# Writing an mLSTM stage with its gate projections ahead of its convolved queries and keys

## Chip, core and metric

The kernel runs on one core of a Trainium2 chip. The metric is device time in microseconds of one execution. Inputs and outputs lie in HBM and are float32; products run on TensorE (PE), elementwise work on VectorE (DVE), ScalarE (ACT) and GpSimd (POOL), and nearly all DMAs are issued from SyncE's queue (SP).

## What is computed

One step of a two-layer decoder trunk, for 1024 new tokens of one prompt and for one new token of each of 8 running sequences (the "samples"). Each layer projects its input `x` (1024 channels) once and feeds three groups of heads: mLSTM (M), retention (R) and HGRN2 (H). Their gated outputs go through one output projection and a LayerNorm.

```
qk        = silu(causal_conv(m_qk))                       # width 4, on the q and k of the mLSTM group
(C, n, m) , h_m = chunked mLSTM(q, k, v, gates)           # matrix memory per head, carried on
y_m       = head_layer_norm(h_m) * sigmoid(m_o) * silu(m_z)
y_r       = head_layer_norm(retention(rope(q), rope(k), v)) * silu(r_g)
y_h       = head_rms_norm(hgrn2(...)) * silu(h_g)
x         = layer_norm(ALPHA * x + W_out [y_m | y_r | y_h])
```

`sigmoid(m_o) * silu(m_z)` are the two gate paths of the mLSTM group. They need only `x`, like every other input projection; what they give is multiplied with the normed heads at the very end.

## The kernel before

The tokens lie along the free dimension, the channels on partitions, and they are worked in two halves: b = 0 holds 512 prompt tokens and the 8 samples (520 columns), b = 1 the other 512. The program writes out, in this order, the stages H, R and M of a half and later its output projection; the stages of the next half lie between. A stage is named here by (layer, half): M of (0, 0), of (0, 1), of (1, 0) and of (1, 1), which is last.

A projection (`project`, L140) makes 128 output channels. Its weights come in two tiles of 256 KB (`load_w`, L126): a DMA, an ACT cast (L133) and a POOL subtraction (L134) split them into a high and a low part; three buffers hold them. Then PE issues 24 products for each run of columns: two runs of 260 columns for b = 0, one of 512 for b = 1. A PSUM tile `pp` (three buffers) takes the sum and a small function `use` evicts it.

The R stage ends with a loop over four chunks of 128 tokens (L474 to L504): transposes (L479, L484), scores (L489), a mask on DVE (L492), outputs (L496, L497), the state (L500, L502), a norm on DVE (L169 to L183, with a power on POOL at L162), and transposes and a product into the gated tile (L206, L212). For b = 0 eight sample steps follow (`sample_R`, L754): each loads a state and two broadcast rows by DMA into `smp` tiles (four buffers), multiplies on POOL (L762), updates on DVE (L763), stores, multiplies on POOL again (L707) and reduces on DVE (L708).

The M stage (`in_M`, L515) has 15 projections. Six give q and k: ACT copies them out (L539), DVE applies the convolution in four passes (L551, three times L553), ACT takes a tanh (L555), DVE finishes the silu (L557), and a DMA moves 32 rows to another tile (L562). `load_x` (L567) then loads the input of the next stage: DMA, ACT cast, DVE subtraction (L157). Three projections give the values (L570). Six are the gate paths, `gate_paths` (L572): an ACT tanh and one DVE operation for each run of columns (L219 and L579). The tiles `tmp` for conv, load and gates come from one ring of four buffers. Four chunks of 128 tokens follow (L591 to L646), beginning with the transposes of values (L604) and keys (L610), and for b = 0 eight sample steps of their own (`sample_M`, L810; L823 and L708 on DVE).

The instruction order on each engine is not that of the text: a scheduler of the tile framework places instructions by readiness and by their place in the program, before the run. At run time each engine takes its instructions strictly in that order. For M of (1, 1) the gate paths are written after the chunks (`final`), in both kernels.

## Time and profile before

| | |
|---|---|
| median of 3 runs | 1415.11 us (1412.8 to 1416.36) |
| the profiled execution | 1413.7 us, span of the core 1411.9 us |
| granted clock of TensorE, mean | 0.968 |
| busy share: PE, DVE, POOL, ACT | 93%, 61%, 54%, 37% |
| products L150 (all projections) | 6192, 1041.9 us busy |

The rows that follow are of five views. The windows give busy time per engine in a stretch. The waits name what an engine stood still for. The table by lines gives count, busy time and mean duration. The timeline lists instructions in order of time, with the idle time before one in square brackets. PE's clock is in tenths of its full 2.4 GHz.

### The profile page before, as it was taken

What the parts mean: (1) busy time and instruction counts of PE and PEld (TensorE: products, weight loads), DVE (VectorE), ACT (ScalarE), POOL (GpSimd) and SP (SyncE); (2) the same over time, 40 slices, a digit from 0 to 9 for tenths busy, and PEclk for the clock granted to TensorE, in tenths of its full rate; (3) what the DMA queues carried; (4) which work ended last, traced back from release to release, by engine and by line L of the source; (5) the groups of instructions that cost most, each with busy time, mean ns of one, the idle gap of its engine ahead of it and who ended that gap; (6) DMA issues with size and microseconds to landing.
All of it is one profiled execution on the core that took longest, in us unless ns stands there. A gap on an engine that the chain in (4) does not pass through costs nothing.

```text
span 1411.9 us, 30603 instructions
## 1 busy us (share of the span) xinstructions
PE 1310.4 (93%) x11888; PEld 1184.0 (84%) x11888; DVE 867.5 (61%) x2120; ACT 522.4 (37%) x1050; POOL 768.0 (54%) x665
## 2 busy tenths in 40 slices
PE   7989998998799999999999999888789999999986
PEld 7889997986698888779978999878678988888886
DVE  4465299369744436828744545974887438484856
ACT  6422322454232233437413333342452333343422
POOL 2455367477633663545554565565764347544664
PEclk9999999998899999999999999999999999999988
DMA  4344244433433442332354444454333334332342
GB/s 151 124 132 133 71 132 130 143 108 114 126 92 106 132 139 73 119 111 63 104 177 120 120 126 120 116 162 132 116 116 106 95 126 142 99 102 94 105 139 90
DMA packets 113257, 166.20 MB, mean 118 GB/s; under 512 B 20516, under 2 KB 49348, under 8 KB 113112
## 3 DMA queue, kind: packets, MB, share of 16 engines
q1 hardware_dynamic: 113112, 164.25, 38.0%
q8 instruction: 93, 1.52, 0.5%
q14 instruction: 52, 0.43, 0.1%
HBM read 140.90 MB, written 15.32 MB: 111 GB/s over the span
## 4 chain that ended last, share of the span: by engine, by line
PE 53%; DVE 17%; DMA 11%; POOL 8%; issue 6%; ACT 3%; SPq 2%; POOLq 0%; ACTq 0%; DVEq 0%
PE pp L150 42%; DMA smp<-drow 4%; POOL w L134 3%; PE pa L371 2%; DVE smp L823 1%; POOL small L162 1%; DVE c L183 1%; DMA out_mC_s_dram<-smp 1%; DVE tmp L553 1%; DMA tmp<-in_xT_dram 1%; DMA st<-in_w_in_dram 1%; DVE x L157 1%; POOL smp L821 1%; DVE mb L618 1%; SPq L735 1%
## 5 line engine op out<-in xcount | busy, mean ns | idle before, releaser
L150 PE MATMUL pp<-x,w 128*128 128x260 f32 (+2 forms) x6192 | 1041.9, 324 | 44.7 <-POOL w L134 21.5
L150 PEld LDWEIGHTS pp<-x,w 128*128 128x128 f32 x6192 | 890.5, 192 | 134.2 <-POOL w L134 28.4
L134 POOL TENSOR_TENSOR w<-st,w 128x512 fp32r<-128x512 f32 x344 | 462.0, 1347 | 390.8 <-ACT w L133 350.3
L133 ACT CAST w<-st 128x512 fp32r<-128x512 f32 x344 | 211.6, 619 | 405.1 <-PE pp L150 270.7
L162 POOL TENSOR_TENSOR small<-small,phalf 128x4 f32<-128x4 f32 (+1 forms) x54 | 62.3, 1154 | 84.6 <-DVE small L195 42.1
L219 DVE SCALAR_TENSOR_TENSOR y<-tmp,pp 128x260 f32<-128x260 f32 (+1 forms) x48 | 24.1, 507 | 72.9 <-ACT tmp L218 72.9
L553 DVE SCALAR_TENSOR_TENSOR tmp<-tmp,prm,tmp 128x544 f32<-128x544 f32 (+1 forms) x72 | 67.9, 944 | 0.6
L707 POOL TENSOR_TENSOR smp<-smp,smp 96x384 f32<-96x384 f32 (+1 forms) x40 | 44.4, 1110 | 20.4 <-DVE smp L763 10.6
L870 DVE SCALAR_TENSOR_TENSOR y<-tmp,pp 128x260 f32<-128x260 f32 (+2 forms) x56 | 25.4, 457 | 42.6 <-PE pp L150 42.1
L386 DVE TENSOR_TENSOR hc<-hc,hg 128x256 f32<-128x256 f32 x48 | 30.4, 633 | 33.0 <-PE pa L371 32.8
L183 DVE TENSOR_SCALAR c<-pa,mv,small 128x96 f32<-128x96 f32 (+1 forms) x144 | 44.2, 367 | 6.5 <-POOL small L162 6.0
L212 DVE SCALAR_TENSOR_TENSOR y<-pf,prm,y 128x128 f32<-128x128 f32 (+1 forms) x132 | 36.4, 325 | 19.3 <-PE pf L206 18.7
L374 DVE COPY_PREDICATED dscores<-lmask,pa 128x128 f32<-128x128 uint8 x96 | 27.3, 298 | 33.4 <-PE pa L371 32.9
L206 PE MATMUL pf<-ident,c 128*128 128x128 f32 (+1 forms) x132 | 30.1, 287 | 16.0 <-DVE c L183 11.6
L555 ACT ACTIVATE tmp<-tmp 128x544 f32<-128x544 f32 (+1 forms) x24 | 15.5, 645 | 75.5 <-DVE tmp L553 54.5
L371 PEld LDWEIGHTS pa<-hc,hc 64*32 64x32 f32 (+1 forms) x2432 | 31.8, 109 | 10.8 <-issue 5.9
L371 PE MATMUL pa<-hc,hc 64*32 64x32 f32 (+1 forms) x2432 | 37.5, 198 | 1.7 <-DVE hc L387 1.7
L904 ACT ACTIVATE t<-pa,small 128x512 f32<-128x512 f32 (+1 forms) x36 | 25.9, 774 | 33.5 <-DVE small L901 33.3
L452 DVE TENSOR_TENSOR x<-pp,tmp 128x260 f32<-128x260 f32 (+1 forms) x36 | 18.1, 511 | 32.5 <-PE pp L150 15.3
L157 DVE TENSOR_TENSOR x<-tmp,x 128x520 fp32r<-128x520 f32 (+1 forms) x32 | 25.2, 806 | 20.8 <-ACT x L156 20.8
L579 DVE SCALAR_TENSOR_TENSOR y<-tmp,y 128x260 f32<-128x260 f32 (+1 forms) x18 | 18.4, 1020 | 29.9 <-ACT tmp L578 29.9
L218 ACT ACTIVATE tmp<-pp 128x260 f32<-128x260 f32 (+1 forms) x48 | 21.8, 457 | 38.2 <-PE pp L150 37.3
(235 smaller groups left out, 1782.6 us busy)
## 6 DMA issues: line engine op xcount, KB each, us to landing
st<-in_w_in_dram SPq DMA_DIRECT2D x280, 256.0 KB
st<-in_w_out_dram SPq DMA_DIRECT2D x72, 256.0 KB
smp<-drow SPq DMA_DIRECT2D x64, 144.0 KB
tmp<-in_xT_dram SPq DMA_DIRECT2D x16, 260.0 KB
tmp<-xres SPq DMA_DIRECT2D x16, 260.0 KB
mb<-db SPq DMA_DIRECT2D x16, 256.0 KB
tmp<-in_xT_dram SPq DMA_DIRECT2D x16, 256.0 KB
xres<-rc SPq DMA_DIRECT2D x16, 256.0 KB
```

The lines of the kernel that those rows point to most:

```text
L133: A.copy(out=w[:, 0], in_=st)
L134: G.tensor_sub(out=w[:, 1], in0=st, in1=w[:, 0].bitcast(F32))
L150: PE.matmul(p, lhsT=w[k // 4][:, wp, k % 4, :], rhs=xt[:, xp, k, c0:c1], start=(k == order[0] and i == 0), stop=(k == order[-1] and i == 2))
L157: eng.tensor_sub(out=xt[:, 1, k, c0:c1], in0=src[:, c0:c1], in1=xt[:, 0, k, c0:c1].bitcast(F32))
L162: G.tensor_tensor(out=r[:n, 0:4], in0=val, in1=phalf[:n], op=ALU.pow)
L183: V.tensor_scalar(out=y[:n, 96 * h:96 * h + 96], in0=ht[:, h, :], scalar1=mv[:n, h, 0:1], scalar2=rs[:n, h:h + 1], op0=ALU.subtract, op1=A ...
L206: PE.transpose(py[:, 128 * j:128 * j + n], y[:n, 128 * j:128 * j + 128], ident[:n, :n])
L212: V.scalar_tensor_tensor(out=dst, in0=py[:, 128 * j:128 * j + n], scalar=prm[:, l, pc + j:pc + j + 1], in1=dst, op0=ALU.mult, op1=ALU.mult)
L371: PE.matmul(pz[z:z + w, i, :], lhsT=k_[r, j, o + z:o + z + w], rhs=q_[r, j, o + z + d:o + z + d + w], start=True, stop=True)
L386: V.tensor_mul(out=hv(Qt, 1), in0=hv(Qt, 1), in1=gv(0))
L553: V.scalar_tensor_tensor(out=acc[:, 0:wc], in0=raw[:, q:q + wc], scalar=cw(q), in1=acc[:, 0:wc], op0=ALU.mult, op1=ALU.add)
L707: G.tensor_mul(out=qb, in0=qb, in1=St)
```

## The change

`gate_paths` and the flag `final` are moved to the head of `in_M`. The call of `gate_paths()` for the three stages that are not the last now stands before the convolution loop; it stood after the values. Nothing is added or left out: on every engine the instructions are the same in kind and number, and only their order differs.

```diff
         ys = [ytile(b, j) for j in range(3)]
+        final = (l, b) == (DEPTH - 1, 1)
+
+        def gate_paths(after=lambda j: None):
+            for j in range(3):
+                project(b, xt, W[t0 + 9 + 2 * j], silu_to(ys[j]))
...
+                project(b, xt, W[t0 + 10 + 2 * j], use)
+                after(j)
+
+        if not final:
+            gate_paths()
         wr = 547 if b == 0 else 515
...
         for j in range(3):
             project(b, xt, W[t0 + 6 + j], copy_to(VV[:, j, :]))
 
-        def gate_paths(after=lambda j: None):
...
-        final = (l, b) == (DEPTH - 1, 1)
         hold = []
-        if not final:
-            gate_paths()
         if b == 0:
             sm = sample_M_pre(l, QH, KH, g), head_columns(VV)
```

Lines of the changed kernel are shifted: L553, L557 and L560 are L570, L574 and L577 there, L579 is L532, and from L589 on a line's number is one higher (L604 is L605, L763 is L764).

The first place is DVE in R's second chunk of (0, 0), from the scores' mask to the eviction of the next projections. In the kernel before the passes of the convolution (`tmp<-tmp,prm,tmp`, `t<-tmp,tmp`) stand between the chunk's steps and the sample steps (`smp`, `shs`):

```order
L553 SCALAR_TENSOR_TENSOR tmp_2838<-tmp_2770,prm,tmp_2838 128x544 x2
L492 TENSOR_TENSOR rc_2505<-pa_2500,cmask 128x512
L183 TENSOR_SCALAR c_304_2475<-pa_2450,mv_2462,small_2473 128x96 x4
L553 SCALAR_TENSOR_TENSOR tmp_2838<-tmp_2770,prm,tmp_2838 128x544
L763 SCALAR_TENSOR_TENSOR smp_2682<-smp_2682,smp_2684 96x384
L541 COPY tmp_2847<-pp_2884 128x8
L548 COPY hist_157<-tmp_2847 128x3
L551 TENSOR_SCALAR tmp_2915<-tmp_2847,prm 128x544
L557 SCALAR_TENSOR_TENSOR t_373_2759<-tmp_2770,tmp_2838 128x512
L560 SCALAR_TENSOR_TENSOR t_373_2759<-tmp_2770,tmp_2838 128x8
L708 TENSOR_REDUCE shs_348_2670<-smp_2683 96x4
```

In the changed kernel the same stretch, from the same mask to the same sample step's reduction, holds chunk steps, sample steps and single evictions of a gate (L532, `y_378`):

```order
L492 TENSOR_TENSOR rc_2505<-pa_2500,cmask 128x512
L183 TENSOR_SCALAR c_304_2475<-pa_2450,mv_2462,small_2473 128x96 x4
L532 SCALAR_TENSOR_TENSOR y_378_2764<-tmp_2868,y_378_2764 128x260
L764 SCALAR_TENSOR_TENSOR smp_2682<-smp_2682,smp_2684 96x384
L532 SCALAR_TENSOR_TENSOR y_378_2764<-tmp_2896,y_378_2764 128x260
L212 SCALAR_TENSOR_TENSOR y_199_1591<-pf_2480,prm,y_199_1591 128x128
L212 SCALAR_TENSOR_TENSOR y_200_1592<-pf_2480,prm,y_200_1592 128x128
L212 SCALAR_TENSOR_TENSOR y_201_1593<-pf_2480,prm,y_201_1593 128x128
L709 TENSOR_REDUCE shs_348_2670<-smp_2683 96x4
```

The six convolutions have left the chunk loop. The second place is where they went, DVE of (0, 0) in the changed kernel; `smp_2748` is the eighth and last sample step of R, `y_380` the last gate tile:

```order
L764 SCALAR_TENSOR_TENSOR smp_2748<-smp_2748,smp_2750 96x384
L532 SCALAR_TENSOR_TENSOR y_380_2766<-tmp_3132,y_380_2766 128x260
L561 COPY tmp_3166<-hist_157 128x3
L709 TENSOR_REDUCE shs_348_2670<-smp_2749 96x4
L532 SCALAR_TENSOR_TENSOR y_380_2766<-tmp_3160,y_380_2766 128x260
L558 COPY tmp_3166<-pp_3203 128x8
L565 COPY hist_157<-tmp_3166 128x3
L568 TENSOR_SCALAR tmp_3234<-tmp_3166,prm 128x544
L561 COPY tmp_3243<-hist_157 128x3
L570 SCALAR_TENSOR_TENSOR tmp_3234<-tmp_3166,prm,tmp_3234 128x544 x3
L574 SCALAR_TENSOR_TENSOR t_373_2759<-tmp_3166,tmp_3234 128x512
```

The whole convolution, six tiles one after another, now stands behind all eight sample steps of R, and nothing else stands between one tile's passes and its silu. The third place is PE in M of (1, 0), at the first chunk of the mLSTM loop. In the kernel before its value transposes (L604) are spread one by one between the gate products of the same stage (`pp` from `x_1069`):

```order
L685 MATMUL pa_12184<-ident,t_1651_11067 8x96
L604 MATMUL pa_12218<-ident,vv_11068 128x128
L150 MATMUL pp_11833<-x_1069_7285,w_11830 128x260 x10
L150 MATMUL pp_11861<-x_1069_7285,w_11825 128x260 x12
L150 MATMUL pp_11861<-x_1069_7285,w_11830 128x260 x12
```

In the changed kernel they stand together behind the last value product, and the first products behind them are those of the next H stage, from the other input tile (`x_1754`, 512 columns):

```order
L686 MATMUL pa_12184<-ident,t_1651_11067 8x96 x2
L605 MATMUL pa_12218<-ident,vv_11068 128x128 x3
L611 MATMUL pa_12223<-ident,t_1650_11066 128x128 x2
L611 MATMUL pa_12223<-ident,t_1651_11067 128x128
L150 MATMUL pp_12651<-x_1754_11934,w_12643 128x512 x12
L150 MATMUL pp_12651<-x_1754_11934,w_12648 128x512 x10
L624 MATMUL pa_12235<-t_1648_11064,t_1650_11066 128x128 x2
```

So that chunk no longer starts under the gates but under the next stage's projections, as it does in (0, 0) in both kernels: from the first L604 of M of (0, 0) on, PE's order there is the same in both.

## Rows read from the trace of the kernel before

**Rows 1.** The page, part 1: busy time, share, instructions
```profile
PE 1310.4 (93%) x11888; PEld 1184.0 (84%) x11888; DVE 867.5 (61%) x2120; ACT 522.4 (37%) x1050; POOL 768.0 (54%) x665
```

**Rows 2.** Windows, (0, 0): length, engines' busy time, PEclk, DMA, GB/s
```profile
200.00:220.00 20.00, 15.90 (x121) 15.16 (x120) 19.69 (x40) 4.54 (x10) 13.70 (x15) 0.91 0.41 130
220.00:240.00 20.00, 15.26 (x122) 14.80 (x123) 17.96 (x48) 7.15 (x16) 12.31 (x12) 0.96 0.38 110
240.00:260.00 20.00, 18.16 (x140) 17.48 (x139) 14.05 (x22) 9.54 (x20) 12.25 (x8) 0.96 0.63 195
260.00:280.00 20.00, 20.00 (x170) 20.00 (x169) 5.50 (x9) 6.66 (x14) 10.32 (x8) 1.00 0.35 106
```

**Rows 3.** Waits of PE, 166 to 290: total us, times, longest
```profile
PE pf L206 <- DVE c L183: 5.0, 3, 3.4
PE pa L489 <- DVE Rst L502: 2.5, 2, 1.9
```

**Rows 4.** Windows, R and M of (1, 0)
```profile
880.00:900.00 20.00, 14.77 (x116) 14.36 (x117) 18.43 (x48) 4.38 (x11) 9.94 (x12) 0.93 0.46 134
900.00:920.00 20.00, 18.32 (x142) 18.11 (x142) 19.66 (x46) 6.34 (x14) 13.62 (x13) 0.90 0.39 108
920.00:940.00 20.00, 16.54 (x110) 15.17 (x108) 19.72 (x30) 7.29 (x15) 14.45 (x13) 0.83 0.48 148
```

**Rows 5.** Waits of PE, 862 to 940
```profile
PE pa L489 <- DVE Rst L502: 4.5, 2, 3.0
PE pp L150 <- DVE tmp L541: 1.7, 1, 1.7
```

**Rows 6.** Waits of PE, 530 to 700, M of (0, 1)
```profile
PE pp L150 <- ACT w L133: 2.3, 1, 2.3
PE pp L150 <- POOL w L134: 1.2, 3, 0.5
```

**Rows 7.** Timeline of PE, (0, 0): R chunk, M chunk, sample heads
```profile
169.38 0.49 PE L479 MATMUL pa<-ident,x 128*128 128x128 f32 x3
...
289.52 0.49 PE L604 MATMUL pa<-ident,vv 128*128 128x128 f32 x3
...
372.41 0.41 PE L830 MATMUL pa<-ident,shs 96*8 96x96 f32 x3
```

**Rows 8.** Timeline of DVE: sample steps of R in (0, 0)
```profile
178.98 0.55 DVE L763 SCALAR_TENSOR_TENSOR smp<-smp,smp 96x384 f32<-96x384 f32 x1
...
223.49 0.55 DVE L763 SCALAR_TENSOR_TENSOR smp<-smp,smp 96x384 f32<-96x384 f32 x1
...
230.78 1.74 DVE L763 SCALAR_TENSOR_TENSOR smp<-smp,smp 96x384 f32<-96x384 f32 x1 [2.04 <-POOL smp L762]
...
246.00 0.54 DVE L708 TENSOR_REDUCE shs<-smp 96x4 f32<-96x384 f32 x1
```

**Rows 9.** By lines, 166 to 290: count, busy us, mean ns, idle
```profile
L134 POOL TENSOR_TENSOR w<-st,w 128x512 fp32r<-128x512 f32 x31 | 43.0, 1387 | 30.7 <-ACT w L133 28.4 <-DMA st<-in_w_in_dram 2.0
...
L553 DVE SCALAR_TENSOR_TENSOR tmp<-tmp,prm,tmp 128x544 f32<-128x544 f32 x18 | 17.2, 958 | 0.1
...
L551 DVE TENSOR_SCALAR tmp<-tmp,prm 128x544 f32<-128x544 f32 x6 | 5.3, 879 | 0.0
...
L557 DVE SCALAR_TENSOR_TENSOR t<-tmp,tmp 128x512 f32<-128x512 f32 x6 | 4.0, 674 | 0.3 <-ACT tmp L555 0.3
...
L555 ACT ACTIVATE tmp<-tmp 128x544 f32<-128x544 f32 x6 | 3.9, 658 | 27.2 <-DVE tmp L553 18.8 <-POOL sconvn L547 8.4
L548 DVE COPY hist<-tmp 128x3 f32<-128x3 f32 x6 | 3.8, 628 | 0.0
```

**Rows 10.** Timeline of DVE: first and last subtractions of the load
```profile
247.57 1.29 DVE L157 TENSOR_TENSOR x<-tmp,x 128x512 fp32r<-128x512 f32 x2
...
257.72 1.97 DVE L157 TENSOR_TENSOR x<-tmp,x 128x512 fp32r<-128x512 f32 x2 [0.34 <-ACT x L156]
```

**Rows 11.** Windows, M chunks of (0, 0)
```profile
330.00:373.00 43.00, 36.14 (x183) 29.00 (x182) 33.87 (x88) 12.47 (x25) 32.79 (x29) 0.92 0.44 126
```

More of the change, by code (lines that the diff above doesn't have):

```diff
@@ L522, in in_M, with use @@
         ys = [ytile(b, j) for j in range(3)]
+        final = (l, b) == (DEPTH - 1, 1)
+        def gate_paths(after=lambda j: None):
+            for j in range(3):
+                project(b, xt, W[t0 + 9 + 2 * j], silu_to(ys[j]))
+                def use(p, c0, c1):
+                    th = tmp()[:, 0:c1 - c0]
+                    A.activation(out=th, in_=p, func=AF.Tanh, scale=0.5)
+                    V.scalar_tensor_tensor(out=ys[j][:, c0:c1], in0=th, scalar=1.0, in1=ys[j][:, c0:c1],
+                                           op0=ALU.add, op1=ALU.mult)
+                project(b, xt, W[t0 + 10 + 2 * j], use)
+                after(j)
+        if not final:
+            gate_paths()
         wr = 547 if b == 0 else 515
@@ L570, in in_M @@
             project(b, xt, W[t0 + 6 + j], copy_to(VV[:, j, :]))
-        def gate_paths(after=lambda j: None):
-            for j in range(3):
-                project(b, xt, W[t0 + 9 + 2 * j], silu_to(ys[j]))
-                def use(p, c0, c1):
-                    th = tmp()[:, 0:c1 - c0]
-                    A.activation(out=th, in_=p, func=AF.Tanh, scale=0.5)
-                    V.scalar_tensor_tensor(out=ys[j][:, c0:c1], in0=th, scalar=1.0, in1=ys[j][:, c0:c1],
-                                           op0=ALU.add, op1=ALU.mult)
-                project(b, xt, W[t0 + 10 + 2 * j], use)
-                after(j)
-        final = (l, b) == (DEPTH - 1, 1)
         hold = []
-        if not final:
-            gate_paths()
         if b == 0:
```

## Prediction

> **What bounds the kernel now.** I read the page first, then the windows of 20 us over the whole span, then PE's waits in the stretches where PE is not full, and last DVE's timeline there. PE is busy 93% of the span [rows 1]. That is the bound, so an order of instructions can only return what PE loses: its idle time, and the time in which its clock is granted below full speed. The windows show where that is. In R and M of (0, 0), DVE is busy 18 to 19.7 of 20 us from 200 to 240, and PE 15 to 16; from 260 on PE is full and DVE has 5.5 us of work [rows 2]. So a DVE-bound stretch (retention chunks, sample steps and convolutions together) is followed by a PE-bound one (the gates). PE's waits there are on DVE, the norm's output and the retention state [rows 3]: one in-order DVE queue serves all three kinds of work late. (1, 0) repeats it from 880 to 940 [rows 4], with the same wait on the state and one on a convolution's eviction [rows 5]. In (0, 1), which has no sample steps, the waits worth a row come to 3.5 us in 170 us, all of it for weights [rows 6].
>
> **The change part by part.** It removes and adds no instruction. It moves 6 of 15 projections: 288 products in a b = 0 stage, 12 weight tiles with their DMAs, casts and subtractions, and the evictions. In front of the convolution loop they lie beside the retention chunks; the convolutions lie behind those.
>
> *R and M of (0, 0).* From the first retention chunk to the first mLSTM chunk PE needs 289.5 - 169.4 = 120.1 us [rows 7]. Its idle time in the three windows is 4.1 + 4.7 + 1.8 = 10.7 us, and the low clock costs 15.90 x 0.09 + 15.26 x 0.04 + 18.16 x 0.04 = 2.8 us [rows 2]. That is 13.5 us of slack: with none, the mLSTM chunk starts at 276.
>
> The new order has a chain of its own on DVE, which I take to be the limit. All eight sample steps now stand ahead of the first convolution. A step's tiles come free only when the step before has stored, so a step waits for DMA and POOL even when DVE is ready: the one at 230.8 stood 2.0 us for POOL's product, 7.3 us after the one before [rows 8]. With 7.3 us a step, the first at 179.0 as now, the eighth is through at 179.0 + 8 x 7.3 = 237; now it ends at 246.5 with most convolutions already done [rows 8]. PE ends its gates earlier and runs ahead by what three `pp` and four `tmp` buffers allow. One convolution tile costs DVE 3 x 0.96 + 0.88 + 0.67 + 0.63 = 5.1 us, and since no other work now stands between its passes and its silu, DVE also waits for ACT's tanh, 0.66 us [rows 9]: 5.7 us. Six give 34 us, to 272. Values and gates cost DVE nothing in this chain. The load's eight subtractions take 12 us from 247.6 [rows 10]; the new order places two ahead of the last tile's silu, so the next stage's input is complete at about 272 + 9 = 281. The mLSTM chunk, which needs q, k and values alone, can start at 276 to 278, and PE's first products from the new input a little later. I take 279, and 10 us gained. The bounds are 13.5 (PE's slack whole) and 0 (the chain below).
>
> What hides the gates' own evictions: 12 single DVE operations under the retention chunks, in place of 6 x 5.1 us of convolution. SP's queue is moved past too: the weight loads of the convolutions stand behind the row moves (L562) that wait for DVE; three weight buffers cover one tile of lag, and I charge it inside the 279.
>
> *R and M of (1, 0).* Idle 5.2 + 1.7 + 3.5 = 10.4 us, clock 14.77 x 0.07 + 18.32 x 0.10 + 16.54 x 0.17 = 5.7 us: 16 us of slack [rows 4]. The same share as above, three quarters, is 12. But here the order of PE shows a loss as well: the first mLSTM chunk ran under the gates and now stands under the next H stage, as in (0, 0). What a stretch of mLSTM chunks without gates costs, (0, 0) shows: 43.0 - 36.14 = 6.9 us idle and 36.14 x 0.08 = 2.9 of clock, 9.8 in all [rows 11]. Some of this (1, 0) pays already; I charge 7. Net gain 5, from -5 to 12.
>
> *(0, 1).* There is almost nothing to win [rows 6], and its first chunk moves in the same way. Without sample steps I charge 2 us, between a gain of 3.5 and a loss of 9.8.
>
> *(1, 1)* keeps its order; nothing is charged.
>
> Sum on the profiled execution: 1413.7 - 10 - 5 + 2 = 1400.7 us. The median of the runs lies 1.4 us above that execution, so the forecast is **1402 us**.
>
> One rule speaks against the change. The step at 230.8 took 1.74 us where the one at 179.0 took 0.55 [rows 8]: an operation on two SBUF tiles sometimes lasts as long as a POOL operation beside it, and the mean pass of 0.96 us contains such cases [rows 9]. The Trainium skill (SBUF — State Buffer, "Who interferes with whom") says that DVE and GpSimd share one port pair as an exclusive lock: a DVE operation with two SBUF inputs waits in full for a GpSimd operation that reads. By that rule a convolution beside nothing but weight subtractions could meet one at every turn. What it would give is the second rival.
>
> **The rivals.**
>
> *All slack returns.* The sample steps run faster once DVE is free, and the clock stays full. For it: DVE is the full engine there, up to 19.7 of 20 us [rows 2], and a late queue delays the sample steps too. Against it: the 2.0 us in which DVE waited for POOL [rows 8]. It gives 1413.7 - 13.5 - 16 + 1.4 = 1386, with a charge of nothing for the chunks; with one of 3 us, 1389.
>
> *The convolution becomes a DVE-bound stage of its own, and nothing is gained.* Two weight subtractions of 1.39 us go with each projection [rows 9]. If each holds up a pass in full, a tile costs 5.7 + 2 x 1.39 = 8.5 us, against 48 x 20 / 170 = 5.6 us of PE for a projection's 48 products (from 260 to 280 PE did 170 of them without a gap [rows 2]). Six tiles take 51 us, to 288: the chunk starts where it did, at 289.5. In (1, 0) the same leaves the 7 us charge against a gain of the like size. That is 1410 to 1417; I put 1413. Against it: the mean of 0.96 already holds such hits, with the sample steps' POOL work on top.
>
> *Slower: the mLSTM chunks lose their cover.* Place: the first chunk of (0, 1) and (1, 0), with the H stage's projections behind it in PE's queue. In both, the chunk's DVE work and the sample steps of (1, 0) fall in a stretch where H's gates and first products also want DVE and POOL. Price: 9.8 us in each [rows 11], and (0, 0) and (1, 0) give back only 5 each: 1413.7 + 19.6 - 10 + 1.4 = 1425. It decides once these two charges exceed what (0, 0) and (1, 0) return. For it: PE waited for hardly anything but weights in (0, 1) while the gates lay there [rows 6]. Against it: (0, 0) runs its chunks uncovered already, and most of DVE's load behind it is unchanged.
>
> **How the numbers follow.** Forecast 0.55 (1394 to 1410), all slack 0.14, nothing gained 0.19, slower 0.12. A difference of 0.3%, 4.2 us, is about what a measurement of this kernel tells from no change, so faster means below 1410.9 and slower above 1419.4. Faster: 0.55 + 0.14 + 0.05 of the third = 0.74; same 0.14; slower 0.12. The range 1390 to 1417 leaves out most of the first rival and the last.
>
> **What would show it.** Right: DVE between the first retention chunk and the last gate clearly below 18 of 20 us, PE's waits on L183 and L502 in rows like [rows 3] mostly gone, the first convolution pass of (0, 0) between 225 and 240, the first L605 near 279 instead of 289.5, and the stretch from there to the sample heads still near 372.4 - 289.5 = 83 us [rows 7]. Wrong: the first L605 at 288 or later with mean passes above 1.2 us (the port), sample steps over 8.5 us apart (the chain), or new waits of PE in the chunks of (0, 1) and (1, 0) of more than 15 us together.

## The result and the profile after

The changed kernel takes 1423.4 us (median of 7 runs, 1421.2 to 1430.7) where the kernel before takes 1416.4 on the same chip (7 runs). The ratio is 1.0055, with a 95% interval of 1.0035 to 1.0076: slower by half a per cent. The forecast was 1402.

The profiled execution took 1421.2 us, 7.5 more than that of before. Part 1 of its page, to be read against [rows 1]:

```profile
PE 1311.5 (92%) x11888; PEld 1184.9 (83%) x11888; DVE 873.8 (62%) x2120; ACT 521.5 (37%) x1050; POOL 750.9 (53%) x665
```

PE's work is the same, 1311.5 us for 1310.4. Its idle time is not: 1419.3 - 1311.5 = 107.8 us for 1411.9 - 1310.4 = 101.5. So 6.3 of the 7.5 us are idle time of PE. To see where, I cut the program at two kinds of DVE instruction that both kernels have: the state update of a stage's first retention chunk (L502), and the score product of its first and its last mLSTM chunk (L625 before, L626 after). The windows between these marks, first of the kernel before (length, busy PE, PEld, DVE, ACT, POOL, granted clock, DMA share, GB/s). In order: (0, 0) from the retention chunk to the first mLSTM chunk, and its mLSTM chunks; the same two of (0, 1); the same two of (1, 0), and from there to the first retention chunk of (1, 1), which holds the H stage of (1, 1).

```profile
178.54:297.57 119.03, 107.75 (x850) 104.27 (x849) 87.10 (x174) 43.90 (x92) 73.91 (x64) 0.97 0.42 128
297.57:361.60 64.03, 56.52 (x272) 44.99 (x271) 54.63 (x132) 28.51 (x46) 46.92 (x41) 0.92 0.42 121
...
539.57:627.30 87.73, 86.53 (x446) 71.58 (x445) 58.65 (x135) 35.91 (x68) 41.52 (x31) 1.00 0.34 104
627.30:682.32 55.02, 54.77 (x440) 52.96 (x439) 43.59 (x119) 33.73 (x64) 25.87 (x22) 1.00 0.23 70
...
867.57:989.56 121.99, 103.76 (x809) 100.18 (x807) 92.62 (x176) 39.45 (x83) 72.75 (x67) 0.94 0.46 132
989.56:1055.78 66.22, 56.13 (x286) 45.34 (x287) 56.37 (x132) 33.94 (x57) 47.03 (x40) 0.95 0.35 108
1055.78:1227.49 171.71, 167.36 (x1810) 145.99 (x1809) 94.39 (x255) 54.62 (x116) 89.82 (x71) 0.98 0.38 120
```

And of the changed kernel:

```profile
179.51:297.72 118.21, 108.58 (x845) 105.41 (x844) 87.29 (x174) 43.17 (x91) 65.30 (x63) 0.96 0.41 124
297.72:362.25 64.53, 54.99 (x277) 42.87 (x276) 55.56 (x131) 29.09 (x47) 47.91 (x43) 0.97 0.44 130
...
540.17:639.10 98.93, 96.70 (x495) 79.43 (x493) 64.71 (x137) 37.87 (x72) 43.05 (x34) 1.00 0.33 99
639.10:689.72 50.62, 46.90 (x389) 46.44 (x389) 43.94 (x119) 31.95 (x61) 23.11 (x20) 0.97 0.20 63
...
874.38:991.31 116.93, 105.83 (x833) 103.25 (x832) 86.38 (x171) 41.30 (x87) 62.86 (x62) 0.96 0.40 122
991.31:1058.17 66.86, 53.37 (x274) 42.56 (x272) 57.50 (x127) 32.12 (x52) 46.55 (x43) 0.95 0.43 129
1058.17:1231.11 172.94, 163.46 (x1783) 142.61 (x1784) 99.21 (x270) 52.42 (x112) 90.93 (x75) 0.96 0.38 119
```

Length less PE's busy time is PE's idle time. (0, 0): 11.3 before and 9.6 after, then 7.5 and 9.5, so nothing came back there. (0, 1): 1.2 and 2.2, then 0.3 and 3.7, and its first mLSTM chunk came 11.2 us later, counted from its first retention chunk. (1, 0): 18.2 and 11.1, a gain of 7, then 10.1 and 13.5, then 4.4 and 9.5: the gain was given back in the mLSTM chunks and in the next H stage. The mark of prediction and trace, the first value transpose of (0, 0), moved by 1.3 us the wrong way, and the sample heads behind it by 0.6; compare [rows 7] (PE's timeline: start, duration):

```profile
290.85 0.49 PE L605 MATMUL pa<-ident,vv 128*128 128x128 f32 x3
...
373.04 0.41 PE L831 MATMUL pa<-ident,shs 96*8 96x96 f32 x3
```

What PE waited for in (0, 0), 170 to 291, against [rows 3]:

```profile
PE pp L150 <- ACT w L133: 3.3, 1, 3.3
PE pa L496 <- DVE rc L492: 2.9, 1, 2.9
PE pp L150 <- POOL w L134: 1.2, 3, 0.5
PE pa L489 <- DVE Rst L502: 1.1, 1, 1.1
PE pf L206 <- DVE c L183: 0.9, 2, 0.5
```

The old waits on L183 and L502 shrank from 7.5 to 2.0 us, and two others grew: those on L133 from 1.3 to 3.3, and those on a retention chunk's score mask, L492, from 0.9 to 2.9. The mask first. Here is what stood ahead of it, on PE, on DVE and on POOL (idle time before an instruction and its releaser in brackets):

```profile
211.63 0.74 PE L496 MATMUL pa<-Rst,x 96*128 96x96 f32 x2 [2.90 <-DVE rc L492]
```

```profile
208.78 0.55 DVE L764 SCALAR_TENSOR_TENSOR smp<-smp,smp 96x384 f32<-96x384 f32 x1 [3.56 <-POOL smp L763]
209.25 0.16 DVE L173 TENSOR_SCALAR small<-mv 128x4 f32<-128x4 f32 x1
210.43 0.55 DVE L709 TENSOR_REDUCE shs<-smp 96x4 f32<-96x384 f32 x1 [1.02 <-POOL smp L708]
210.90 0.68 DVE L492 TENSOR_TENSOR rc<-pa,cmask 128x512 f32<-128x512 f32 x1
```

```profile
207.92 0.82 POOL L763 TENSOR_TENSOR smp<-smp,svs 96x384 f32<-96x384 f32 x1 [3.47 <-DMA smp<-drow]
```

PE waits for DVE's mask, the mask stands in DVE's queue behind a sample step, the step waits for POOL, and POOL for the transfer of the step's rows. DVE is not busy here, it is stuck. In the kernel before it was full instead, and hardly ever stuck. This is what DVE waited for POOL's product of a retention sample step from 170 to 250, before and after (us in all, times, longest):

```profile
DVE smp L763 <- POOL smp L762: 2.3, 2, 2.0
```

```profile
DVE smp L764 <- POOL smp L763: 15.2, 6, 3.6
```

The time that the convolution left free on DVE became waiting for the steps, and what stands behind a step in DVE's queue waits with it.

### The profile page after: what moved, and what is told of

The parts are those of the page before. It is cut to its first block, busy times and chain, and to the rows that moved or that the text cites. A ratio compares the mean times of both kernels' runs of the same rounds, so it can differ in the third digit from the quotient of the medians.

```text
span 1419.3 us, 30584 instructions
## 1 busy us (share of the span) xinstructions
PE 1311.5 (92%) x11888; PEld 1184.9 (83%) x11888; DVE 873.8 (62%) x2120; ACT 521.5 (37%) x1050; POOL 750.9 (53%) x665
## 4 chain that ended last, share of the span: by engine, by line
PE 54%; DVE 17%; DMA 11%; POOL 7%; issue 6%; ACT 2%; SPq 2%; POOLq 0%; ACTq 0%; DVEq 0%
PE pp L150 43%; DMA smp<-drow 5%; DVE tmp L570 3%; POOL w L134 3%; PE pa L371 2%; DMA out_ret_s_dram<-smp 1%; POOL smp L708 1%; SPq L736 1%; PE pf L206 1%; PE pa L896 1%; DVE x L157 1%; PE pa L409 1%; POOL small L162 1%; DVE small L180 1%; DVE t L907 1%
## 5 line engine op out<-in xcount | busy, mean ns | idle before, releaser
L134 POOL TENSOR_TENSOR w<-st,w 128x512 fp32r<-128x512 f32 x344 | 455.4, 1328 | 398.9 <-ACT w L133 319.4
L133 ACT CAST w<-st 128x512 fp32r<-128x512 f32 x344 | 212.1, 618 | 427.3 <-PE pp L150 276.7
L162 POOL TENSOR_TENSOR small<-small,phalf 128x4 f32<-128x4 f32 (+1 forms) x54 | 55.5, 1028 | 97.9 <-DVE small L195 41.9
L570 DVE SCALAR_TENSOR_TENSOR tmp<-tmp,prm,tmp 128x544 f32<-128x544 f32 (+1 forms) x72 | 74.7, 1038 | 1.7
L219 DVE SCALAR_TENSOR_TENSOR y<-tmp,pp 128x260 f32<-128x260 f32 (+1 forms) x48 | 24.3, 506 | 67.4 <-ACT tmp L218 67.4
L183 DVE TENSOR_SCALAR c<-pa,mv,small 128x96 f32<-128x96 f32 (+1 forms) x144 | 44.2, 368 | 10.4 <-POOL small L162 9.7
L206 PE MATMUL pf<-ident,c 128*128 128x128 f32 (+1 forms) x132 | 31.3, 293 | 17.8 <-DVE c L183 11.9
L212 DVE SCALAR_TENSOR_TENSOR y<-pf,prm,y 128x128 f32<-128x128 f32 (+1 forms) x132 | 36.4, 327 | 18.1 <-PE pf L206 17.3
L371 PEld LDWEIGHTS pa<-hc,hc 64*32 64x32 f32 (+1 forms) x2432 | 31.7, 109 | 11.2 <-issue 6.3
L206 PEld LDWEIGHTS pf<-ident,c 128*128 128x128 f32 (+1 forms) x132 | 17.9, 154 | 24.1 <-DVE c L183 14.8
L452 DVE TENSOR_TENSOR x<-pp,tmp 128x260 f32<-128x260 f32 (+1 forms) x36 | 18.2, 512 | 30.6 <-PE pp L150 18.8
```

The costliest lines, as they stand in the source:

```text
L133: A.copy(out=w[:, 0], in_=st)
L134: G.tensor_sub(out=w[:, 1], in0=st, in1=w[:, 0].bitcast(F32))
L162: G.tensor_tensor(out=r[:n, 0:4], in0=val, in1=phalf[:n], op=ALU.pow)
L183: V.tensor_scalar(out=y[:n, 96 * h:96 * h + 96], in0=ht[:, h, :], scalar1=mv[:n, h, 0:1], scalar2=rs[:n, h:h + 1], op0=ALU.subtract, op1=A ...
L206: PE.transpose(py[:, 128 * j:128 * j + n], y[:n, 128 * j:128 * j + 128], ident[:n, :n])
L212: V.scalar_tensor_tensor(out=dst, in0=py[:, 128 * j:128 * j + n], scalar=prm[:, l, pc + j:pc + j + 1], in1=dst, op0=ALU.mult, op1=ALU.mult)
```

## The experiments

A single profiled execution is a weak witness here. In the first run below, the order on PE and DVE is the same as in the changed kernel up to 529 us, yet it is 7 us later by then. So I go by ratios with their intervals, and by idle times over several kernels that share an order in the stage in question.

**One stage at a time.** `gate_paths()` is called early only where the flag says so, and behind the values elsewhere:

```diff
-        if not final:
+        early = (l, b) == (0, 0)        # then (0, 1) alone, then (1, 0) alone
+        if early:
             gate_paths()
...
+        if not final and not early:
+            gate_paths()
```

(0, 0) alone. Expected:

> The gate paths stand first in stage (0,0) alone; the other stages are written as before. Theory A (each stage pays for itself; by offsets between the two traces (0,0) gained nothing: its first mLSTM chunk came at 290.85 us instead of 289.52, 1.0 of which was there before its retention part began): 1414 to 1418 us, ratio 0.998 to 1.002. Theory B (the 6.8 us that (0,1) loses are handed to it by (0,0), whose late load of x and late chunks push into it): 1420 to 1423 us. Theory C (the prediction's own: a gain of 10): 1405 to 1408.

Measured: 1424.0 us, ratio 1.0046 (1.0028 to 1.0064). (0, 0), on which the forecast set its largest gain, costs time by itself. That is near B's time, but not as B has it: (0, 1) idles 1.3 us in this run, no more than in the kernel before. A and C had (0, 0) lose nothing.

(0, 1) alone. Expected:

> The gate paths stand first in stage (0,1) alone. Theory A (the stage itself loses: the first mLSTM chunk waits for six gate projections more, and the chunks then run with nothing beside them): 1421 to 1425 us, ratio 1.004 to 1.006, and TensorE busy less than 9.3 of 10 us in the chunk stretch. Theory B (the loss is handed on from (0,0)): 1414 to 1418. The prediction gave this edit a loss of 2: 1417 to 1419.

Measured: 1421.8 us, 1.0036 (1.0017 to 1.0055): theory A's time, so B falls. But PE is busy 46.1 of 47.7 us in the chunk stretch, where A asked for less than 9.3 of 10: A's reason, chunks that run with nothing beside them, is not borne out.

(1, 0) alone. Expected:

> The gate paths stand first in stage (1,0) alone. Theory A (gain of the stage 3.5 us, and the 3.6 us lost in (1,1) are not tied to it but to an instruction order that every version draws anew): 1411 to 1414 us, ratio 0.996 to 0.999. Theory D (the loss in (1,1) follows from the gates-first order of (1,0), whose sample steps run 34 to 44 us later): 1415 to 1418, ratio 0.999 to 1.002, with the retention chunks of (1,1) late against before by 3 us or more.

Measured: 1417.2 us, 1.0013 (0.9996 to 1.0030). The time is theory D's. The retention chunks of (1, 1) came 5.5 to 8.4 us late in its profile, but the first one of (1, 0) was 5.1 us late already, so this sign says little. For D's place speaks the stretch ahead of the retention chunk of (1, 1): 9.5 us of idle time instead of 4.4.

**(0, 0) and (1, 0) without (0, 1).** The same flag with two stages. Expected:

> Gate paths first in (0,0) and (1,0), not in (0,1). Theory A (each stage pays for itself; (0,1) alone cost 5.1 us, ratio 1.0036): 4 to 6 us below the changed kernel, 1417 to 1420, ratio 1.000 to 1.003. Rival (the stages' prices don't add, and (0,0) alone with its 6.5 us holds all of the loss): 1421 to 1425, ratio 1.004 to 1.006. In (0,0) the order is that of the changed kernel, so its idle time should be the same as there, 18 to 22 us from the first retention chunk to the last mLSTM chunk.

Measured: 1421.4 us, 1.0029 (1.0008 to 1.0051); the time lies in the rival's range, the ratio in theory A's, so this run does not decide between them. The three stages alone add up to 0.95%, all three together cost 0.55%: with these intervals the prices need not add.

PE's idle time in us from these runs, each window's length less PE's busy time, as means over kernels with the same order in that stage (gates behind: the kernel before and those runs that leave the stage as it was; gates first: the changed kernel and those that move them):

| stretch | gates behind | gates first |
|---|---|---|
| (0, 0), retention chunk to mLSTM chunk | 9.5 (8.2 to 11.3, 5 kernels) | 11.4 (9.6 to 12.4, 3) |
| (0, 0), mLSTM chunks | 9.1 (7.5 to 10.0, 5) | 9.2 (8.5 to 9.5, 3) |
| (0, 1), the same two | 1.4 (1.1 to 1.7, 5) | 5.0 (4.1 and 5.9, 2) |
| (1, 0), retention chunk to mLSTM chunk | 17.3 (16.5 to 18.2, 4) | 10.7 (10.3 to 11.1, 3) |
| (1, 0), mLSTM chunks | 9.3 (8.3 to 10.2, 4) | 14.4 (13.5 to 15.6, 3) |
| from there to the retention chunk of (1, 1) | 4.6 (3.7 to 5.4, 4) | 9.6 (9.5 to 9.7, 3) |

One stretch gains 6.6, four lose, by 1.9, 3.6, 5.1 and 5.0, and one stays. The sum is +9, and the rest of this section asks why.

Idle time is not all of it. From the first retention chunk of (0, 0) to that of (0, 1), PE runs 2963 instructions in each of these kernels. With the gates behind this takes 359.2 us on the mean (357.4 to 361.7, 5 kernels), with the gates first 364.2 (360.7 to 367.6, 3). Of the 5.0 us, 2.5 are idle time; in the other 2.5 PE is busy, at a mean granted clock of 0.953 instead of 0.962.

**Whose slack was it in (0, 0)?** The retention's sample steps of layer 0 are reduced to passing the state through, in the kernel before and in the changed one:

```diff
                 dma(out=St, in_=I["s_ret"][l, h, hf])
+                if l == 0:
+                    dma(out=O["ret_s"][l, h, hf], in_=St)
+                    if h == hf == 0:
+                        G.memset(hs[0:96], 0.0)
+                    continue
```

Before. Expected:

> The kernel before, without the arithmetic and the row transfers of the retention's eight sample steps in layer 0 (states pass through, the read is set to zero); the base for the next run. Theory R (a good part of TensorE's idle time beside the retention chunks of (0,0) comes from these steps, which stand in VectorE's queue and wait for GpSimd and its transfers): idle from the first retention chunk of (0,0) to the first mLSTM chunk at most 6 us instead of 8 to 11, 1400 to 1410 us. Theory V (the prediction's: it comes from the convolution's passes on VectorE): idle stays at 8 us or more, 1408 to 1416.

After. Expected:

> The changed kernel, without the same steps, to be read against the run before this one. Theory V: with only the convolution left to hold the chunks up, moving it away pays: 5 us or more below that run. Theory R: the slack was the steps', so there is nothing left to gain, and the changed kernel stays 2 to 10 us above that run, as it does with the steps.

Measured: 1406.2 us (0.9961, 0.9940 to 0.9981) and 1415.0 us (1.0014, 0.9994 to 1.0034). The first windows of (0, 0), of before and of after without the steps:

```profile
183.58:284.09 100.51, 98.04 (x829) 97.04 (x828) 65.44 (x159) 42.26 (x88) 46.80 (x45) 1.00 0.33 107
```

```profile
184.46:290.01 105.55, 103.11 (x845) 101.61 (x844) 69.25 (x157) 43.73 (x91) 50.20 (x47) 0.98 0.31 100
```

PE's idle time is 2.5 and 2.4 us, where it was 9.5 and 11.4. In the kernel before the convolutions still lie beside the retention chunks, and with the steps gone they cost PE next to nothing. The slack goes with the steps, wherever the convolution lies. The windows from 200 to 220 show how little DVE's busy time says: first of the changed kernel with the steps, then of the kernel before without them; [rows 2] has the kernel before with them.

```profile
200.00:220.00 20.00, 15.97 (x110) 15.55 (x109) 14.88 (x43) 5.05 (x10) 10.87 (x11) 0.83 0.35 105
```

```profile
200.00:220.00 20.00, 20.00 (x177) 20.00 (x176) 18.05 (x60) 9.00 (x18) 9.51 (x10) 1.00 0.17 57
```

With DVE busy for 14.88 us PE idles 4.0; with DVE busy for 18.05 it does not idle at all. Theory R holds on both counts, and theory V, the prediction's, falls. The changed kernel stays above, by 1.0014 / 0.9961 = 1.0053, the same half per cent as with the steps: they explain why there was nothing to gain, not why the changed kernel is slower. And the edit takes the steps' work from DVE, POOL and the DMA queue together; which of the three held PE up is not shown.

**The convolution behind the retention part.** The six convolved projections of (0, 0) in the changed kernel use the high part of the weights twice, so that POOL has no subtraction to do for them:

```diff
-                project(b, xt, W[t0 + 2 * j + qk], use)
+                project(b, xt, W[t0 + 2 * j + qk], use, low=(l, b) != (0, 0))
```

Expected:

> The changed kernel, but the six convolved projections of (0,0) leave out the low part of their weights: GpSimd's subtraction is not issued and the high part is multiplied in its place, so TensorE's work is the same. Theory P (the convolution is a VectorE chain of 6.7 us a tile, 2 of them because one of three passes takes 1.7 to 1.86 us instead of 0.79 and the 3-element history copy 1.1 instead of 0.17 while GpSimd subtracts): 4.6 to 5.2 us a tile, the last pass of (0,0) by 272 instead of 276.6, the first mLSTM chunk at 285 or earlier, 1414 to 1418 us in all. Theory Q (the end of the stage is set by TensorE's three value projections, whose weight casts sit behind the casts of the x load on ScalarE): the tiles get shorter but the first chunk stays within 2 us of 290.9 and the time within 3 us of 1423.

In the changed kernel a tile looks like this on DVE (the three passes of a tile stand in one row):

```profile
252.22 1.11 DVE L565 COPY hist<-tmp 128x3 f32<-128x3 f32 x1
253.24 0.55 DVE L568 TENSOR_SCALAR tmp<-tmp,prm 128x544 f32<-128x544 f32 x1
...
253.83 3.51 DVE L570 SCALAR_TENSOR_TENSOR tmp<-tmp,prm,tmp 128x544 f32<-128x544 f32 x3
258.14 0.69 DVE L574 SCALAR_TENSOR_TENSOR t<-tmp,tmp 128x512 f32<-128x512 f32 x1 [0.81 <-ACT tmp L572]
```

Without the subtractions (lines shifted by one):

```profile
251.33 0.16 DVE L566 COPY hist<-tmp 128x3 f32<-128x3 f32 x1
251.53 0.56 DVE L569 TENSOR_SCALAR tmp<-tmp,prm 128x544 f32<-128x544 f32 x1
...
252.12 2.43 DVE L571 SCALAR_TENSOR_TENSOR tmp<-tmp,prm,tmp 128x544 f32<-128x544 f32 x3
255.87 0.69 DVE L575 SCALAR_TENSOR_TENSOR t<-tmp,tmp 128x512 f32<-128x512 f32 x1 [1.32 <-ACT tmp L573]
```

A pass takes 0.79 us alone, and in five of the six tiles one of the three takes 1.7 to 1.9 beside a subtraction; a copy of three elements takes 1.1 instead of 0.16. Tiles come 6.0 us apart on the mean instead of 6.7, and the first value transpose at 286.6 instead of 290.9: P's mechanism, if less of it than P named, and more than Q allowed. But the time is 1423.1 us (1.0049, 1.0018 to 1.0080), as Q had it; with five executions a gain of 4 us would not show. By the Trainium skill (SBUF — State Buffer, "Who interferes with whom") DVE and GpSimd share a port pair as an exclusive lock that the first to issue keeps for its whole instruction, and copies are among the operations that can take it. The trace agrees: the 1.11 us above are a copy of three columns, and it ends with this subtraction, which began 0.25 us before it:

```profile
251.97 1.33 POOL L134 TENSOR_TENSOR w<-st,w 128x512 fp32r<-128x512 f32 x1 [2.00 <-issue]
```

**The history copies on ScalarE.** Both `V.tensor_copy` of the history become `A.copy`, in the kernel before and in the changed one.

Before. Expected:

> The kernel before, with the two three-column history copies of each convolved tile (in: history into the tile, out: the tile's last columns into the history) on ScalarE instead of VectorE. It is the base for the next run and a candidate. Theory P (VectorE's history copy takes 1.1 us instead of 0.17 where GpSimd subtracts, and VectorE holds TensorE up beside the retention chunks): 1408 to 1413 us. If VectorE has room there, or ScalarE's queue delays the copies as much: 1414 to 1419.

After. Expected:

> The changed kernel with the same two history copies on ScalarE. Theory P (in (0,0) the convolution alone sets the pace behind the retention part, 6.7 us a tile of which the copy is 1.1): a tile of (0,0) 5.5 to 5.8 us apart, the last pass by 272, 1415 to 1419 us, a larger gain than the same edit brings to the kernel before. Rival (the pace of (0,0) is TensorE's own work and its waits for weights and sample steps): under 2 us of gain, 1421 to 1425.

Measured: 1421.8 us (1.0035, 1.0012 to 1.0057) and 1422.9 us (1.0044, 1.0021 to 1.0066). No gain in either (the first is above both of its forecasts), and the tiles of (0, 0) still came 6.4 us apart; P falls as an account of the time. The wait had only moved on, to the next operation, in the changed kernel's (0, 0):

```profile
256.04 1.18 DVE L568 TENSOR_SCALAR tmp<-tmp,prm 128x544 f32<-128x544 f32 x1
```

**The load of the next input.** The other new wait of PE, 3.3 us on L133, has the load ahead of it in ACT's queue:

```profile
276.40 0.62 ACT L156 CAST x<-tmp 128x512 fp32r<-128x512 f32 x1 [3.71 <-DMA tmp<-in_xT_dram]
277.85 0.62 ACT L156 CAST x<-tmp 128x512 fp32r<-128x512 f32 x1 [0.82 <-DMA tmp<-in_xT_dram]
278.37 0.61 ACT L133 CAST w<-st 128x512 fp32r<-128x512 f32 x1
```

So in (0, 0) the load's tiles were taken from another ring (`t = mb() if (l, b) == (0, 1) else tmp()` in `load_x`, whose arguments name the input's own layer and half). Expected:

> The changed kernel, but the tiles of the x load in (0,0) come from the ring of mb instead of tmp, so that they don't wait for the convolution's tiles and the load is done beside the gate projections. Theory Q (in (0,0) the casts of the x load, which wait for their transfers on ScalarE, hold up the weight casts of the value projections and the last tanh): TensorE's wait for a weight cast of 3.3 to 3.8 us near 279 is gone, the first mLSTM chunk comes 3 us or more earlier than 297.7 and TensorE's idle time from the first retention chunk to it is at most 7; 1418 to 1421 us. Theory P (the stage is a VectorE chain, and the load's eight subtractions only move ahead of the convolution): the idle time stays at 9 to 12 us, 1422 to 1426.

Measured: 1427.6 us, 1.0084 (1.0061 to 1.0107). The wait on L133 there is down to 0.2 us, but PE's idle time up to the first mLSTM chunk rose to 12.9, and that chunk came 4.9 us later, counted from the first retention chunk: the load now lies ahead of the convolutions, whose first pass comes at 252.4 instead of 240.6. Q falls; P comes nearer, and both its forecasts are passed.

**The mLSTM's sample steps in (1, 0).** In the kernel before they are added to their states from 961 us on, four of the eight ahead of the chunks' first mark at 989.6. In the changed kernel they run from 996 on, beside the chunks and into the next H stage (DVE; before the first and the last of the eight, after the first and the seventh, with the eighth at 1064.5):

```profile
961.39 1.64 DVE L823 TENSOR_TENSOR smp<-smp,smp 96x384 f32<-96x384 f32 x1 [0.72 <-POOL smp L821]
...
1026.76 1.65 DVE L823 TENSOR_TENSOR smp<-smp,smp 96x384 f32<-96x384 f32 x1
```

```profile
995.81 0.54 DVE L824 TENSOR_TENSOR smp<-smp,smp 96x384 f32<-96x384 f32 x1
...
1056.31 1.20 DVE L824 TENSOR_TENSOR smp<-smp,smp 96x384 f32<-96x384 f32 x1 [1.99 <-POOL smp L822]
...
1057.57 0.67 DVE L219 SCALAR_TENSOR_TENSOR y<-tmp,pp 128x512 f32<-128x512 f32 x1
```

L219 at 1057.57 is an eviction of the H stage of (1, 1), and it stands behind a step that waits for POOL. PE waits for it, the longest wait of the last stretch:

```profile
PE pp L150 <- DVE y L219: 6.4, 1, 6.4
```

Three runs try whether the steps explain the loss. First, one pair of gate projections early in (1, 0) instead of three. Expected:

> Only in stage (1,0), and only one of the three pairs of gate projections stands ahead of the convolution; the other two stay behind the values. With all three pairs TensorE's idle time between the first retention chunk and the first mLSTM chunk fell from about 17.5 to 10.3 us, and rose by 5 in the mLSTM chunks and by 5 in the stretch behind them. Theory S (what is lost later comes from the sample steps of the mLSTM, which start only when queries and keys are convolved and stand in VectorE's queue ahead of the chunks' work and of the evictions of the next stage; a third of the delay costs less than a third): idle 13 to 16 in the first stretch, at most 10 and 6 in the next two, 1411 to 1414 us. Theory L (each projection taken from behind the values is cover taken from the chunks, one for one): 1415 to 1418, no gain.

Measured: 1420.0 us, 1.0019 (0.9999 to 1.0038). Idle times of the three stretches: 11.3, 12.0 and 9.8, the first and the last as with three pairs, the middle one halfway. The steps begin at 991: one pair is enough to send them behind. That is neither a third of the gain nor a third of the loss, so the dose decides nothing and both theories miss.

Then the steps of layer 1 without their arithmetic, with gates behind and with gates first in (1, 0) (the edit is that of the retention's steps, with `l == 1` in `sample_M`). Expected:

> The kernel before, without the arithmetic of the mLSTM's eight sample steps in layer 1 (the states pass through unchanged, the read is set to zero). It is the base for the next run. All theories: 1406 to 1415 us, as these steps load GpSimd and VectorE beside the gate projections.

Expected:

> Gate paths first in (1,0) alone, without the arithmetic of the mLSTM's eight sample steps in layer 1, to be read against the run of the kernel before without them. Theory S: with the steps gone the gain of the stage is kept: 3 to 8 us below that run, and the wait of 6.1 to 6.4 us of TensorE for a silu eviction (near 1058 us in the changed kernel) is gone. Theory L: no gain or a loss against that run, minus 1 to plus 3 us, since the chunks still run without gate projections beside them.

Measured: 1399.2 us (0.9879, 0.9856 to 0.9903), below the 1406 to 1415 that was expected of the base, and 1398.4 us (0.9874, 0.9857 to 0.9891). The first two stretches of (1, 0), gates behind, then gates first:

```profile
868.33:982.42 114.09, 104.85 (x811) 102.31 (x810) 82.89 (x172) 39.49 (x84) 63.58 (x58) 0.91 0.49 143
982.42:1030.50 48.08, 48.08 (x268) 40.38 (x267) 42.01 (x114) 30.32 (x50) 22.68 (x20) 1.00 0.22 67
```

```profile
872.16:991.80 119.64, 108.94 (x833) 105.22 (x833) 84.47 (x172) 41.07 (x87) 62.77 (x62) 0.94 0.48 139
991.80:1046.10 54.30, 51.08 (x271) 42.12 (x270) 43.39 (x121) 30.12 (x49) 27.45 (x25) 0.97 0.25 77
```

Without steps the kernel before idles 9.2 us in the first stretch instead of 17.3, and not at all in the chunks. So 8 of the 17 us of idle time, and all of the chunks', were the steps'. With gates first it idles 10.7 and 3.2, and 5.2 instead of 9.6 in the stretch behind. The 6.4 us wait is gone, as S said, but the gain of 3 to 8 is not there: the two times are equal within their intervals, which is theory L's forecast. So the 6.6 us that the first stretch gains with the steps in place are about the 8 that the steps cost there: moved behind, they come back as 5.1 and 5.0. A gain that would be left without the steps is not shown.

**(0, 1) with one pair left behind the values.** Expected:

> Only in (0,1), two of the three gate pairs ahead of the convolution and one behind the values. Theory K (the loss is the cover that the mLSTM chunks of (0,1) lose: some 48 us of VectorE work against 0 us of projections, with one pair left 9 us of them beside the chunks): the first mLSTM chunk 6 to 8 us later than before instead of 10.5 to 11.8, TensorE idle less than 2.5 us in that stage, 1417 to 1420 us. Rival (any gate pair ahead costs the same, by the order that it draws in the retention chunks): 1420 to 1424.

Measured: 1422.3 us, 1.0036 (1.0016 to 1.0057), the same as with all three ahead. The idle times are 2.9 and 2.1 us, and from the stage's first retention chunk to its first mLSTM chunk it takes 98.7 us, 11 more than before (87.7), as with three (98.9). K falls; the rival's time came.

**Does any new order lose?** Two neutral reorderings of the kernel before: the key tile ahead of the query tile in each pair, and all queries ahead of all keys.

```diff
-            for qk, tl in ((0, QH), (1, KH)):
+            for qk, tl in ((1, KH), (0, QH)):
```

Expected:

> The kernel before, with the convolved key tile of each pair written ahead of the query tile: the same operations on every engine, another order. Theory N (the order of before is a lucky one, and whatever makes the planner draw another loses 3 to 6 us): 1419 to 1423 us. Theory G (the loss belongs to the moved gate projections): 1414 to 1418.

Expected (queries, then keys):

> The kernel before, with all three query tiles convolved ahead of the three key tiles: the same operations, an order that differs in more places than in the run before this one. Theory N: 1419 to 1423 us. Theory G: 1414 to 1418.

Measured: 1414.4 us (1.0000, 0.9975 to 1.0024) and 1417.0 us (1.0035, 1.0016 to 1.0054; before 1414.1 in this comparison). Both times are theory G's. By the ratios one reordering is free, the other costs a third of a per cent, like the history copies on ScalarE. So not every order loses, but 0.35% can come from an order alone, and a part of the 0.55% may be no more than that. This was not separated. The granted clock goes with it: 0.9676 on the mean of the free one's 12 executions, 0.9634 for the other's 12, and 0.9665 for the 35 of the kernel before.

**A version that beats both.** If the sample steps hold the stages with samples up, and POOL waits there for rows because a step takes three `smp` tiles of four, a larger ring should help where the gates did not:

```diff
-NBUF = dict(..., c15=6, smp=4, ...)
+NBUF = dict(..., c15=4, smp=6, ...)     # then c15=5, smp=5
```

Expected (six):

> A candidate to beat both: the kernel before (gate paths behind the values) with six instead of four buffers for the sample steps' tiles, and four instead of six in the c15 ring to make room. Theory R (the slack of the stages with samples belongs to the sample steps: GpSimd waits 2 to 4 us at a time for the next step's rows, since a step takes three tiles and only one more is free): GpSimd's waits for row transfers in (0,0) fall below 5 us in all, TensorE's idle time from the first retention chunk of (0,0) to the first mLSTM chunk to 3 to 7 us instead of 8 to 11, 1406 to 1411 us. Rival (the two buffers taken from c15 are missed in the chunks, or the redrawn order costs as much): 1414 to 1421.

Expected (five):

> The same with five buffers for the sample steps' tiles and five in the c15 ring. Theory R: a part of the gain of the run with six, 1409 to 1414 us. Rival: 1414 to 1420.

Measured: 1408.4 us (0.9956, 0.9934 to 0.9978) and 1404.2 us (0.9925, 0.9897 to 0.9954), both faster than both kernels. In (0, 0) of the version with six, from 170 to 250, POOL waits 0.2 us for the rows' transfers (`drow`); in the kernel before it is 8.9, in the changed one 15.9. But the idle time that this was to end, in (0, 0) up to the first mLSTM chunk, is 11.0 and 11.9 us, not 3 to 7. So the row transfers, the last link of the chain in the section above, are not what this idle time hangs on with the gates behind, and why the versions are faster is only located: 9.1 and 10.6 us of idle time instead of 17.3 in (1, 0), and 1.6 and 1.3 instead of 6.1 behind the mLSTM chunks of (0, 0). That five would do as well as six was not foreseen; their intervals overlap. The larger ring with the gates first was not run.

## Why the prediction was wrong

**The failed step** is the reading of the slack: "a DVE-bound stretch (retention chunks, sample steps and convolutions together)". From it followed that DVE's work, taken out of the stretch, comes back as PE's time. A window says that DVE is busy 18 to 19.7 of 20 us [rows 2]; it doesn't say whose work holds PE. In the changed kernel DVE is busy 14.9 us from 200 to 220 and PE idles as before, while DVE's waits for POOL's sample products, from 170 to 250, rose from 2.3 to 15.2 us. Without the retention's sample steps, and with the convolutions in place, the idle time of (0, 0) is 2.5 us. Most of the slack of 13.5 us goes with these steps, and in (1, 0) 8 of the 17 us of idle time with those of the mLSTM; the change lightens neither.

**R and M of (0, 0), gain 10.** Measured alone: a loss of 0.46%. The chain up to the convolution came out as worked: steps 7.4 us apart on the mean (forecast 7.3), the last through at 237.6 (237), first pass at 240.6. What the sum left out is that the retention chunks' work for PE stands behind these waiting steps in the same queue. Three of its signs of being right even came: DVE well below 18 of 20 us (14.9 and 13.3 from 200 to 240), the waits on L183 and L502 mostly gone, 82.2 us from the first L605 to the sample heads. They spoke of DVE and of two waits, not of PE's idle time. A tile then took 6.7 us, not 5.7: the mean pass 1.07 us instead of 0.96, the history copy 1.08 instead of 0.63. These two rows are of 170 to 291, against [rows 9]:

```profile
L570 DVE SCALAR_TENSOR_TENSOR tmp<-tmp,prm,tmp 128x544 f32<-128x544 f32 x18 | 19.2, 1065 | 0.5
L565 DVE COPY hist<-tmp 128x3 f32<-128x3 f32 x6 | 6.5, 1084 | 0.0
```

The six tiles ended at 282 instead of 272. The mis-sized tile is 6 us of the 12 by which the first chunk missed its 279. The second rival, the convolution as a stage of its own, described this place well, with 6.7 us a tile between the forecast's 5.7 and its 8.5. But shorter tiles (6.0 us) brought no gain in time that could be seen, so the term is not shown to be the cause.

**(1, 0), gain 5.** The retention stretch gained 6.6 us of idle time where the forecast had 12 with the clock. The charge of 7 for the chunks was too small: 5.1 in the chunks and 5.0 in the H stage behind them, which no step of the forecast looked at. Net: 1.0013, within the noise of nothing.

**(0, 1), loss 2.** Measured alone: 0.36%, some 5 us; its first chunk was some 11 us late and 3.6 us of idle time were new. The third rival had the direction and nearly the time, 1425. It asked for 15 us of new waits in the chunks of (0, 1) and (1, 0); the idle time there rose by 3.5 + 3.4 = 6.9. Its mechanism, chunks that lose their cover, is not shown: with one pair of gates left beside the chunks (0, 1) lost as much.

**The granted clock** was charged as a loss that goes away with the waits. It did not: 0.967 in the profiled execution, as before (0.968). Over more executions it lies lower: 0.964 on the mean of the changed kernel's seven, and 0.9635 with the gates first in (0, 1) alone (12 executions) beside 0.9661 for the kernel before in the same comparison (27). On 1310 us of PE's work that last difference is an estimated 1310 x 0.0026 = 3.4 us, of the 5 that this run costs.

**Still open:** why the changed kernel is slower at all, and not just no faster. (0, 0) alone loses 0.46%. In its stretch half of the 5 us were idle time and half PE's busy time at a lower clock, on the mean of three profiles. But between two executions with the same order the clock in the mLSTM chunks of (0, 0) was 0.97 and 0.90, so these profiles can't settle it, and a part may be the order alone.

## What to carry to other kernels

A full engine in a window is a suspect, not a culprit: follow one wait of the bounding engine back through every queue to the instruction that is itself waiting, here a sample step that waits for POOL, and ask whether the edit touches that. Leaving one suspect out of the kernel before is one run: without the sample steps, and with the convolution in place, PE idled 2.5 us, so there was little for the convolution to give back. And when work moves ahead, list what now moves behind, past the end of the stage too: one pair of gate projections was enough to send eight sample steps behind, the last of them into the next stage.

## What the runs showed of the hardware

- Two profiled executions with one order of instructions on PE and DVE up to 529 us stood 7 us apart by then. The same stretch, the mLSTM chunks of (0, 0), in the changed kernel above had a clock of 0.97; in the run with (0, 0) alone:

```profile
301.27:368.75 67.48, 58.03 (x277) 47.74 (x276) 57.56 (x132) 29.09 (x47) 47.13 (x42) 0.90 0.43 125
```

- The mean granted clock of whole executions went with the order of the same instructions: 0.9634 (12 executions, queries then keys) and 0.9665 (35, the kernel before), for a ratio of 1.0035.
- A copy of three elements a partition on DVE took 1.1 us beside a POOL subtraction and 0.16 without. Taken off DVE, it passed its wait on to the next operation (0.55 to 1.18 us).
- Taking the mLSTM's eight sample steps out of layer 1 was worth 17 us (1.2%), those of the retention in layer 0 0.4%.
